# Expert-weighted token copies: the products split between VectorE and ScalarE, loads issued from within ScalarE's products, and half of the output stored in smaller pieces

## The chip, the cores and the metric

The kernel runs on one NeuronCore of a Trainium2 chip. The metric is the device time of one execution in microseconds (us). Thirteen runs of the kernel before gave a median of 240.83 us (240.25 to 242.64). The core has compute engines with their own instruction queues (the profile names them PE, DVE for VectorE, ACT for ScalarE, POOL, SP for SyncE) and 16 DMA engines that move data between HBM and the on-chip memory SBUF (128 partitions). A DMA is issued by an engine's queue; here SP and ScalarE issue all of them, and the profile shows their transfers as the DMA queues q1 (those issued by SP) and q10 (those issued by ScalarE).

## What is computed

Every token's hidden vector is copied k = 2 times, and each copy is multiplied by that slot's expert weight. The expert indices are not used.

```python
batch, seq, hidden, k = 16, 1024, 512, 2        # x, weights and output are float32
x_expanded = x[:, :, np.newaxis, :].repeat(k, axis=2)
weights = expert_weights[..., np.newaxis]
return (x_expanded * weights).astype(np.float32)
```

So 33.6 MB are read (x), 67.1 MB are written, and there is one multiplication per output element: 16,384 tokens by 2 slots by 512 elements.

## The kernel before, in words

The 16,384 tokens are taken in eight groups of 2,048. In a group, partition p holds 16 consecutive tokens (TX = 16), so that a load of a group is one DMA of 128 rows of 32 KB (4 MB in all, line 70), and one buffer of `x_tile` holds it. `x_pool` has two buffers. The weights of a group are a 128 x 32 block; all eight blocks are loaded ahead of everything else by eight small DMAs that SP issues (line 55; 16 KB each, in rows of 128 bytes), into one `w_tile`.

For each of the 16 tokens of a partition VectorE makes two products of shape 128 x 512 (line 83, a `tensor_scalar` multiplication whose scalar is a column of `w_tile`): one for slot 0, one for slot 1. They go into `o_tile`, which holds eight tokens (TO = 8) of 2 x 512 elements, 32 KB a partition. After eight tokens SP issues one store of that tile (line 91, 128 rows of 32 KB, 4 MB). `o_pool` has four buffers, so four stores can be outstanding. A whole run has 8 loads of x, 256 products and 16 stores.

The order is set by four things:

- VectorE works through the products in order. The first product of a group waits for that group's load; the first product of an output tile waits until the store that last used the buffer has landed.
- ScalarE's queue holds nothing but the eight loads (line 70). Load i+2 waits until VectorE has finished the products of group i, whose buffer it takes.
- SP's queue holds the eight weight loads and then the stores, in order. Each store waits for its tile's last product.
- The DMAs share eight completion semaphores, numbered 0 to 7 here, handed out in the order in which the scheduler places the DMAs. A DMA whose semaphore was used before waits until that earlier DMA has landed. So the eighth weight load waits for the first load of x, the second load of x waits for the first weight load, and the first stores wait for weight loads.

On each DMA engine a queue is worked through in its order, one row after another: a row of 32 KB is one packet in the trace. Where both queues have packets, the packets of the two alternate.

Of the kernel before, what the change touches and what calls it, by code (L numbers as in the profile page):

```python
# [1 line left out]

# [4 lines left out]


@with_exitstack
def kernel(  # L10
    ctx: ExitStack,
    tc: tile.TileContext,
    x: bass.AP,
    expert_indices: bass.AP,
    expert_weights: bass.AP,
    out: bass.AP,
):
    nc = tc.nc

    batch, seq, hidden = x.shape  # L20
    k = expert_weights.shape[-1]
    P = nc.NUM_PARTITIONS
    ntok = batch * seq
    assert ntok % P == 0
    A_TOTAL = ntok // P

    f32 = mybir.dt.float32
    row = k * hidden
    TX = 16
    TO = 8  # L30

    groups = [[[16]], [[16]], [[16]], [[16]], [[16]], [[16]], [[16]], [[16]]]
    assert sum(sum(sum(t) for t in g) for g in groups) == A_TOTAL

    xf = x.rearrange("b s h -> (b s) h")
    of = out.rearrange("b s k h -> (b s) (k h)")
    wf = expert_weights.rearrange("b s k -> (b s) k")

    w_pool = ctx.enter_context(tc.tile_pool(name="w_pool", bufs=1))
    x_pool = ctx.enter_context(tc.tile_pool(name="x_pool", bufs=2))
    o_pool = ctx.enter_context(tc.tile_pool(name="o_pool", bufs=4))

    w_tile = w_pool.tile([P, A_TOTAL * k], f32)

    def rows(of_all, done, T):
        return of_all[done * P : (done + T) * P, :].rearrange(
            "(p a) n -> p (a n)", a=T
        )  # L50

    done = 0
    for group in groups:
        T = sum(sum(t) for t in group)
        nc.sync.dma_start(
            out=w_tile[:, done * k : (done + T) * k], in_=rows(wf, done, T)
        )
        done += T

    done = 0  # L60
    for group in groups:
        T = sum(sum(t) for t in group)
        xr = rows(xf, done, T)
        outr = rows(of, done, T)
        a0 = 0
        for pieces in group:
            x_tile = x_pool.tile([P, TX * hidden], f32)
            at = 0
            for n in pieces:
                nc.scalar.dma_start(  # L70
                    out=x_tile[:, at * hidden : (at + n) * hidden],
                    in_=xr[:, (a0 + at) * hidden : (a0 + at + n) * hidden],
                )
                at += n
            ends = [sum(pieces[: i + 1]) for i in range(len(pieces))]
            first = 0
            for t in range(at):
                if t % TO == 0:
                    o_tile = o_pool.tile([P, TO * row], f32)
                for kk in range(k):  # L80
                    c = (done + a0 + t) * k + kk
                    o = t % TO * row + kk * hidden
                    nc.vector.tensor_scalar(  # L83
                        out=o_tile[:, o : o + hidden],
                        in0=x_tile[:, t * hidden : (t + 1) * hidden],
                        scalar1=w_tile[:, c : c + 1],
                        scalar2=None,
                        op0=mybir.AluOpType.mult,
                    )
                if t + 1 in ends or (t + 1) % TO == 0:  # L90
                    nc.sync.dma_start(
                        out=outr[:, (a0 + first) * row : (a0 + t + 1) * row],
                        in_=o_tile[:, first % TO * row : (t % TO + 1) * row],
                    )
                    first = t + 1
            a0 += at
        done += T


# [1 line left out]
_INS = ['x', 'expert_indices', 'expert_weights']  # L101
_OUTS = [((16, 1024, 2, 512), 'float32')]


# [23 lines left out]
```

## Time and profile before

| what | value |
|---|---|
| median of 13 runs | 240.83 us |
| time of the profiled execution | 240.83 us |
| its span, first to last instruction | 239.0 us |
| VectorE busy | 102.5 us, 43% of the span |
| one product, 128 x 512 | 481 ns; successive ones start 396 ns apart |
| bytes moved | 100.81 MB, mean 422 GB/s over the span |
| VectorE idle, waiting for stores to free a buffer | 74.9 us in 10 waits |
| VectorE idle, waiting for a load of x | 25.4 us in 2 waits |
| first product starts | 13.32 us |
| first store issued | 19.77 us |
| last store issued | 206.08 us |

How to read it: the span of one profiled execution lies 1.8 us below that execution's time, which is what lies around the first and last instruction. The time from an issue to the landing of a DMA holds its wait in the queue behind earlier DMAs as well as its own transfer: the median is 45.1 us for a store and 24.0 us for a load of x. The row of GB/s and the row of the DMA engines' busy share divide the span into 40 slices of 6 us.

### The profile page before, as it was taken

To read this page: it belongs to the slowest core of one execution; us is meant where nothing else is said; L and a number is where in the kernel's file an instruction comes from. 1 tells how busy PE (TensorE), PEld (TensorE's weight loads), DVE (VectorE), ACT (ScalarE), POOL (GpSimd) and SP (SyncE) were. 2 spreads that over 40 slices of the span, in tenths; PEclk is the share of its full clock that TensorE was granted. 3 is DMA by queue.
4 is the path that set the end of the run, shared out by engine and by line. 5 is a ranking of instruction groups with operands and counts; after the bars stand their busy time and mean duration, and the time that the engine had idled before them with its cause. 6 is when DMAs were issued, how large, how long until landed. Compare 5 with 4: busy or idle time off the path is not lost.

```text
span 239.0 us, 369 instructions
## 1 busy us (share of the span) xinstructions
DVE 102.5 (43%) x256; POOL 0.2 (0%) x4
## 2 busy tenths in 40 slices
DVE  0079994058700904672055910749008485400000
POOL 0000000000000000000000000000000000000000
DMA  7999999999999999999999999999999999999995
GB/s 266 440 440 400 417 429 389 433 439 439 433 422 433 422 439 439 439 428 433 428 439 433 439 428 439 439 435 422 433 422 428 439 433 428 439 433 439 433 439 225
DMA packets 4610, 100.81 MB, mean 422 GB/s; under 512 B 1536, under 2 KB 1536, under 8 KB 1536
## 3 DMA queue, kind: packets, MB, share of 16 engines
q1 hardware_dynamic: 3456, 67.24, 65.4%
q10 hardware_dynamic: 1152, 33.55, 33.2%
q14 instruction: 2, 0.02, 0.0%
HBM read 33.69 MB, written 67.11 MB: 422 GB/s over the span
## 4 chain that ended last, share of the span: by engine, by line
DMA 62%; DVE 18%; another core or an unknown queue 5%; issue 0%; DVEq 0%
DMA out_dram<-o_tile 56%; DVE o_tile L83 18%; DMA x_tile<-in_x_dram 5%; DVEq L123 0%; DVEq L83 0%
## 5 line engine op out<-in xcount | busy, mean ns | idle before, releaser
L83 DVE TENSOR_SCALAR o_tile<-x_tile,w_tile 128x512 f32<-128x512 f32 x256 | 102.5, 481 | 103.5 <-DMA out_dram<-o_tile 74.9
L112 POOL MEMSET const-bfloat16-1.0<- 128x1 bf16 x1 | 0.1, 101 | 0.0
L112 POOL MEMSET const-uint8-127<- 128x1 uint8 x1 | 0.1, 101 | 0.0
L112 POOL MEMSET const-float32-0.0<- 128x1 f32 x1 | 0.1, 98 | 0.2 <-issue 0.2
L112 POOL MEMSET const-float32-1.0<- 128x1 f32 x1 | 0.1, 98 | 0.0
## 6 DMA issues: line engine op xcount, KB each, us to landing
out_dram<-o_tile SPq DMA_DIRECT2D x16, 4096.0 KB, 45.1
x_tile<-in_x_dram ACTq DMA_DIRECT2D x8, 4096.0 KB, 24.0
w_tile<-in_expert_weights_dram SPq DMA_DIRECT2D x8, 16.0 KB, 20.7
```

The source lines that it names most:

```text
L83: nc.vector.tensor_scalar(out=o_tile[:, o : o + hidden], in0=x_tile[:, t * hidden : (t + 1) * hidden], scalar1=w_tile[:, c : c + 1], scala ...
L112: nc = _bacc.Bacc("TRN2", target_bir_lowering=False, num_devices=1)
```

## The change

Seven things are different in the new kernel:

- The product of slot 0 stays on VectorE (line 85), that of slot 1 is made by ScalarE (line 79, `nc.scalar.mul` with the same column of weights as its multiplier). Each has 128 products of 128 x 512. ScalarE also gets a load of its function table ahead of its first product.
- The 16 tokens of a group now go out in three stores in place of two: two of four tokens (128 rows of 16 KB, 2 MB each) and one of eight tokens (128 rows of 32 KB, 4 MB). There are 24 stores in place of 16.
- The pool of four 32 KB output buffers becomes a pool of four 16 KB buffers (`half_pool`) and a pool of two 32 KB ones (`o_pool`): the same bytes in all.
- The loads of x have the same size as before and are still issued by ScalarE, now with its products between them. The first two are issued at the start; load i+1 stands behind ScalarE's first product of group i.
- A load also waits for ScalarE's own products on the buffer it takes, and stores and buffers wait for both engines.
- With more DMAs, the eight completion semaphores fall to other DMAs. The first three stores now wait for the second, third and fifth weight load, and the next two for the sixth and eighth.
- The loops over lists of pieces are replaced by plain ones. The weight loads are as before.

```diff
     x_pool = ctx.enter_context(tc.tile_pool(name="x_pool", bufs=2))
-    o_pool = ctx.enter_context(tc.tile_pool(name="o_pool", bufs=4))
+    half_pool = ctx.enter_context(tc.tile_pool(name="half_pool", bufs=4))
+    o_pool = ctx.enter_context(tc.tile_pool(name="o_pool", bufs=2))
...
+    loaded = []
+    def load():
+        i = len(loaded)
+        if i < G:
+            loaded.append(x_pool.tile([P, TX * hidden], f32, name="x_tile"))
+            nc.scalar.dma_start(out=loaded[i], in_=rows(xf, i))
+    load()
+    load()
+    for i in range(G):
+        x_tile = loaded[i]
+        at = 0
+        for pool, m in ((half_pool, TO // 2), (half_pool, TO // 2), (o_pool, TO)):
+            o_tile = pool.tile([P, m * row], f32, name="o_tile")
+            for t in range(m):
                 for kk in range(k):
...
-                    nc.vector.tensor_scalar(
-                        out=o_tile[:, o : o + hidden],
-                        in0=x_tile[:, t * hidden : (t + 1) * hidden],
-                        scalar1=w_tile[:, c : c + 1],
-                        scalar2=None,
-                        op0=mybir.AluOpType.mult,
-                    )
-                if t + 1 in ends or (t + 1) % TO == 0:
-                    nc.sync.dma_start(
-                        out=outr[:, (a0 + first) * row : (a0 + t + 1) * row],
-                        in_=o_tile[:, first % TO * row : (t % TO + 1) * row],
-                    )
+                    if kk == 1:
+                        nc.scalar.mul(
+                            out=o_tile[:, o : o + hidden],
+                            in_=in_,
+                            mul=w_tile[:, c : c + 1],
+                        )
+                    else:
+                        nc.vector.tensor_scalar(
+                            out=o_tile[:, o : o + hidden],
+                            in0=in_,
+                            scalar1=w_tile[:, c : c + 1],
+                            scalar2=None,
+                            op0=mybir.AluOpType.mult,
+                        )
+                if i > 0 and at == 0 and t == 0:
+                    load()
+            nc.sync.dma_start(
+                out=rows(of, i)[:, at * row : (at + m) * row], in_=o_tile
+            )
+            at += m
```

More of the change, by code (lines that the diff above doesn't have):

```diff
@@ L30 @@
     TO = 8
-    groups = [[[16]], [[16]], [[16]], [[16]], [[16]], [[16]], [[16]], [[16]]]
-    assert sum(sum(sum(t) for t in g) for g in groups) == A_TOTAL
+    G = A_TOTAL // TX
+    assert A_TOTAL % TX == 0 and TX == 2 * TO
     xf = x.rearrange("b s h -> (b s) h")
@@ L42 @@
     x_pool = ctx.enter_context(tc.tile_pool(name="x_pool", bufs=2))
-    o_pool = ctx.enter_context(tc.tile_pool(name="o_pool", bufs=4))
-    w_tile = w_pool.tile([P, A_TOTAL * k], f32)
-    def rows(of_all, done, T):
-        return of_all[done * P : (done + T) * P, :].rearrange(
-            "(p a) n -> p (a n)", a=T
-        )
-    done = 0
-    for group in groups:
-        T = sum(sum(t) for t in group)
-        nc.sync.dma_start(
-            out=w_tile[:, done * k : (done + T) * k], in_=rows(wf, done, T)
-        )
-        done += T
@@ L60 @@
[L60 to L79, printed above, removed]
-                for kk in range(k):
-                    c = (done + a0 + t) * k + kk
-                    o = t % TO * row + kk * hidden
-                    nc.vector.tensor_scalar(
-                        out=o_tile[:, o : o + hidden],
-                        in0=x_tile[:, t * hidden : (t + 1) * hidden],
-                        scalar1=w_tile[:, c : c + 1],
-                        scalar2=None,
-                        op0=mybir.AluOpType.mult,
-                    )
-                if t + 1 in ends or (t + 1) % TO == 0:
-                    nc.sync.dma_start(
-                        out=outr[:, (a0 + first) * row : (a0 + t + 1) * row],
-                        in_=o_tile[:, first % TO * row : (t % TO + 1) * row],
[L94 to L97, printed above, removed]
@@ new lines, with rows @@
+    half_pool = ctx.enter_context(tc.tile_pool(name="half_pool", bufs=4))
+    o_pool = ctx.enter_context(tc.tile_pool(name="o_pool", bufs=2))
+    def rows(of_all, g):
+        return of_all[g * P * TX : (g + 1) * P * TX, :].rearrange(
+            "(p a) n -> p (a n)", a=TX
+        )
+    w_tile = w_pool.tile([P, A_TOTAL * k], f32)
+    for g in range(G):
+        nc.sync.dma_start(out=w_tile[:, g * TX * k : (g + 1) * TX * k], in_=rows(wf, g))
+    loaded = []
[4 more added lines that the diff above has]
+            nc.scalar.dma_start(out=loaded[i], in_=rows(xf, i))
@@ new lines @@
+    load()
[6 more added lines that the diff above has]
+            for t in range(m):
+                for kk in range(k):
+                    c = (i * TX + at + t) * k + kk
+                    o = t * row + kk * hidden
+                    in_ = x_tile[:, (at + t) * hidden : (at + t + 1) * hidden]
+                    if kk == 1:
[16 more added lines that the diff above has]
+                out=rows(of, i)[:, at * row : (at + m) * row], in_=o_tile
+            )
+            at += m
```

## The prediction

> **What bounds the kernel now.** I read the page's busy shares first, then the bandwidth by slices, then the waits, and last a table of stretches.
>
> ```profile
> span 239.0 us, 369 instructions
> DVE 102.5 (43%) x256; POOL 0.2 (0%) x4
> ...
> DMA  7999999999999999999999999999999999999995
> GB/s 266 440 440 400 417 429 389 433 439 439 433 422 433 422 439 439 439 428 433 428 439 433 439 428 439 439 435 422 433 422 428 439 433 428 439 433 439 433 439 225
> DMA packets 4610, 100.81 MB, mean 422 GB/s; under 512 B 1536, under 2 KB 1536, under 8 KB 1536
> q1 hardware_dynamic: 3456, 67.24, 65.4%
> q10 hardware_dynamic: 1152, 33.55, 33.2%
> DMA 62%; DVE 18%; another core or an unknown queue 5%; issue 0%; DVEq 0%
> ```
>
> The only computing engine is busy 43% of the time; the 16 DMA engines are busy in every slice but the first and last, and q1 and q10 together take 98.6% of them. The chain of waits puts 18% on VectorE, but only because it follows one thread back; while those products ran, the DMA engines were full with other stores. The waits agree: VectorE waits for DMAs.
>
> ```profile
> DVE o_tile L83 <- DMA out_dram<-o_tile: 74.9, 10, 12.9
> DVE o_tile L83 <- DMA x_tile<-in_x_dram: 25.4, 2, 13.3
> DVE o_tile L83 <- issue: 3.2, 1, 3.2
> ```
>
> The stretches (from:to, length, VectorE, POOL, clock, DMA share, GB/s) show where anything can be won:
>
> ```profile
> 0.00:4.00 4.00, 0.00 (x0) 0.20 (x4) 1.00 0.65 216
> 4.00:20.00 16.00, 6.68 (x17) 0.00 (x0) 1.00 1.02 436
> 20.00:25.00 5.00, 5.00 (x14) 0.00 (x0) 1.00 0.96 360
> 25.00:34.00 9.00, 9.00 (x24) 0.00 (x0) 1.00 1.03 445
> 34.00:39.00 5.00, 4.74 (x12) 0.00 (x0) 1.00 0.96 347
> 39.00:92.00 53.00, 19.27 (x48) 0.00 (x0) 1.00 1.00 433
> 102.00:180.00 78.00, 32.12 (x80) 0.00 (x0) 1.00 1.00 433
> 180.00:236.00 56.00, 19.27 (x48) 0.00 (x0) 1.00 1.00 432
> ```
>
> From 39 us to 236 us the rate is 432 to 433 GB/s, whether loads and stores are mixed (39 to 92) or stores run alone (180 to 236). That is the ceiling: 100.8 MB at 433 GB/s are 232.8 us, and the span is 239.0. The missing 6.2 us lie at the ends: about 2 us before full rate (0 to 4), 5 x (1 - 360/433) = 0.8 us in 20 to 25, 5 x (1 - 347/433) = 1.0 us in 34 to 39, 2.7 us after 236, less 0.4 us where the count of bytes by packets runs above the ceiling. The profiled execution's own time is 240.83 us, equal to the median of the 13 runs, so 1.83 us lie around the span and sums made on the span go over to the median unchanged.
>
> **The change, part by part.**
>
> *Slot 1 to ScalarE.* VectorE loses 128 of 256 products, 128 x 0.40 us (start to start) = 51 us of work. None was on the path: the DMA engines are full beside it. On ScalarE 128 products appear. The trace has no such row. A group's DMA work is 12.6 MB / 433 GB/s = 29.1 us and holds 16 of these products, so ScalarE becomes the bound only above 29.1/16 = 1.8 us each. From below, VectorE's 0.40 us for the same shape; from above, four times that, 1.6 us, a far end that I choose for want of a nearer row. I take the geometric mean, 0.8 us. Both ends are below 1.8, so the steady part costs 0. The table load stands behind the second load's issue (8.4 us) and ahead of the first product (13.3 us): it has 4.5 us of cover. The Trainium skill ("ScalarE: Activation LUTs", Rules for kernel authors) speaks against this part: multiplications belong on VectorE; by its figures, 280 ns plus 0.833 ns an element with one operand more read per partition, my estimate of a product is 0.71 us. By the skill a group takes 11.3 us on ScalarE and the sum would still be 0.
>
> *Loads behind products.* Before, load i+1 was issued when VectorE had finished group i-1 (38.77, 64.48, 99.60 us and so on). Now it stands behind ScalarE's first product of group i, which waits for load i and for the landing of the first half store of group i-2. At that moment the rest of group i-2 and all of group i-1 are still to be stored: 6.3 + 8.4 = 14.7 MB, 34 us of DMA time. A load that shares the engines takes the 24.0 us of its row, probably less, since its 32 KB packets now alternate with 16 KB ones in half of the stores. So the store queue never empties behind a late load: 0. Queued behind the waiting load's product on ScalarE are the other products of group i; they have the same 34 us of cover.
>
> *24 stores for 16.* SP's issues take 0.33 us each, 8 x 0.33 = 2.7 us more, on a queue that waits 177.8 us for VectorE: 0. What counts is the price on the DMA engines, which have no slack. The packet records of the trace give a median of 1213 ns for a 32,768-byte packet, 13 ns for a 128-byte one and 9 ns for a 4-byte semaphore write. A straight line through the first two gives 13 + 16,256 x 0.03676 = 611 ns for 16,384 bytes. Sixteen half stores have 128 such packets on each engine in place of 64 large ones: 128 x 611 - 64 x 1213 = 0.53 us, and eight more DMAs add eight semaphore writes: 0.07 us. Together +0.6 us. From below: exactly half a packet each, 0. From above: the weight loads that drain alone land 0.2 us apart with nine packets each (22.57, 22.77, 22.97, 23.19, 23.40 us for the first semaphore step of five of them), 22 ns a packet; 64 + 8 more packets at that price are 1.6 us. I take the line, because the large stream keeps its packets back to back and the small one did not. The Trainium skill ("DMA: Bandwidth & Descriptors", Anatomy of one DMA) speaks harder against it, with 2.0 us of fixed cost for every DMA: by that rule, laid end to end, eight more would cost 16 us. The trace contradicts it for queued DMAs: the last four 4 MB stores land 9.7 us apart (209.20, 218.87, 228.56, 238.23 us), and 4.19 MB at 433 GB/s are 9.69 us, which leaves no room for a fixed cost.
>
> *The head.* A half tile has its four products on ScalarE at about 13.3 + 4 x 0.8 = 16.5 us in place of 19.77. That brings nothing: in the trace of before no store packet moves until 22.53 us, though the first store was issued at 19.77, since the weight loads' small packets stand ahead of it on q1, alternating with 32 KB packets of x until those run out, from 22 us on. The first half store is then 8 x 0.61 = 4.9 us of DMA work on each engine, to 27.4 us at the earliest, where the 4 MB store before covered 9.7. The second half store has its products at 13.3 + 8 x 0.8 = 19.7 us but waits on the semaphore of the third weight load, which landed at 23.83 us: 3.6 us ahead of need. Then come the 4 MB store (fifth weight load, 24.18 us; products at 13.3 + 16 x 0.8 = 26.1 us) and the third load of x, behind ScalarE's first product of group 1 (about 26.9 us; before, 26.11). I cost the head at 0; its cover is this 3.6 us.
>
> *The tail.* The last store is again 4 MB and queued long before its turn. Ahead of it stand three stores of group 6 and two of group 7, 29 us of work, when its buffer comes free; its products need 8 x 0.8 = 6.4 us. 0.
>
> Sum: 240.83 + 0.6 = 241.4 us, +0.25%, with 0 to +1.6 from the packets.
>
> **Rivals.**
>
> *Dearer packets (slower).* The 16 KB packets cost the 22 ns overhead of the draining weight loads. For: that is the only row with many packets in a row. Against: they were tiny, and 32 KB packets at 433 GB/s leave no gap. 240.83 + 1.6 = 242.4 us. It decides from 10 ns a packet on, where the cost passes 0.3%.
>
> *The store queue runs dry in the head (slower).* A DMA that joins busy engines starts late: the third load was issued at 26.11 us and moved its first packet at 30.1. If the second half store needs the same 4.0 us, it starts at 27.8, 0.4 us after the first can end; if it starts only with the 4 MB store behind it (26.1 + 4.0 = 30.1), 2.7 us are lost. The middle, 1.6 us, gives with the packets 243.0. Against: on the same queue the next packets are fetched behind the running ones, and 19.77 to 22.53 was blocking, not latency.
>
> *ScalarE becomes the bound (slower).* Above 1.8 us a product; at 2.0 us each, 128 x 2.0 = 256 us plus a start of 13 and an end of 10: 279 us. Nothing in the trace speaks for it.
>
> *The head gets better (faster).* The dips of 20 to 25 and 34 to 39 us (0.8 + 1.0 us) are not explained by any wait: packets of x there took up to 2.3 us in place of 1.2. If they come from the pattern of 4 MB against 4 MB and vanish, 240.83 + 0.6 - 1.8 = 239.6 us. It decides once more than 1.3 us of the 1.8 are won. Against: similar slow packets come at the very start, where only loads run.
>
> **How the numbers follow.** My forecast has 0.56, dearer packets 0.19, a dry queue 0.09, ScalarE 0.03, the better head 0.13. A change under 0.3% (0.72 us) is about what a measurement of this kernel cannot tell from none. The forecast's own range is 240.8 to 242.0 (packets 0 to 1.2 us); of its 0.56 I put 0.13 above 241.55, where it counts as slower. So slower 0.13 + 0.19 + 0.09 + 0.03 = 0.44, same 0.43, faster 0.13. The range from 240.1 to 243.0 leaves out half of the better head, ScalarE, and some of the dry queue: under 2 in 10.
>
> **What will show it.** In the changed profile: 432 to 433 GB/s from 40 us to the last 3 us; 128 ScalarE products between 0.4 and 1.6 us; VectorE near 51 us of busy time start to start (61.6 at 481 ns each); the two large queue shares together still 98% or more; 16 KB packets at 611 ns. A slice below 8 tenths of DMA between 20 and 40 us would show the dry queue. I am wrong if the ceiling itself moves, for instance if 16 KB rows are written at another rate than 32 KB rows, since nothing in this trace wrote such rows.

## The result and the profile after

The changed kernel takes 244.89 us in the median (243.5 to 249.0) against 240.98 us (240.16 to 243.18) for the kernel before: a ratio of 1.0142, 95% interval 1.0115 to 1.0170. The ratio leaves out the run of 249.0 us, which is more than 1.5% above the fastest. The forecast was 241.4 us in a range of 240.1 to 243.0: the sign of the likeliest case was right, the size was not, and the median lies above the range. The profiled execution took 244.55 us with a span of 242.8; so 1.75 us lie around the span (1.83 before), and what is to be explained is 242.8 - 239.0 = 3.8 us of span.

The first lines of the changed kernel's page, its two computing engines, and its waits (engine, line, what was waited for: total us, times, longest):

```profile
span 242.8 us, 406 instructions
...
DVE 52.4 (22%) x128; ACT 81.8 (34%) x129; POOL 0.2 (0%) x4
...
DMA  7999999999999999999999999999999999999992
GB/s 267 428 434 351 443 440 413 443 432 418 400 470 431 439 432 397 440 405 437 410 424 440 421 427 397 429 448 432 437 410 432 454 413 429 454 413 429 454 432 108
...
q1 hardware_dynamic: 4608, 67.24, 65.1%
q10 hardware_dynamic: 1152, 33.55, 32.9%
...
L79 ACT ACT_TABLE_LOAD x1 | 1.3, 1283 | 8.7 <-DMA w_tile<-in_expert_weights_dram 8.7
```

```profile
L79 ACT ACTIVATE o_tile<-x_tile,w_tile 128x512 f32<-128x512 f32 x128 | 80.5, 709 | 117.7 <-DMA out_dram<-o_tile 113.5 <-DMA x_tile<-in_x_dram 4.0
```

```profile
DVE o_tile L85 <- DMA out_dram<-o_tile: 117.1, 12, 18.5
ACT o_tile L79 <- DMA out_dram<-o_tile: 113.5, 13, 17.6
```

Much of this is as foretold. The DMA engines are busy in every slice but the first and the last, the two large queues together take 98.0% of the 16 engines' span, and both computing engines wait for stores to free their buffers. A product takes 709 ns on ScalarE, and ScalarE is busy 34% of the time. No slice between 20 and 40 us falls below 9 tenths, so the store queue didn't run dry. Yet the same bytes need 3.8 us more.

Where they are lost is seen in the windows (from:to, length, VectorE, ScalarE where it computes, POOL, clock, DMA share, GB/s). Before:

```profile
0.00:25.00 25.00, 11.68 (x30) 0.20 (x4) 1.00 0.95 385
25.00:40.00 15.00, 13.74 (x35) 0.00 (x0) 1.00 1.01 411
40.00:180.00 140.00, 57.82 (x144) 0.00 (x0) 1.00 1.00 433
180.00:236.00 56.00, 19.27 (x48) 0.00 (x0) 1.00 1.00 432
236.00:239.00 3.00, 0.00 (x0) 0.00 (x0) 1.00 0.13 55
```

And after:

```profile
0.00:25.00 25.00, 7.52 (x19) 12.15 (x19) 0.20 (x4) 1.00 0.94 370
25.00:40.00 15.00, 5.33 (x14) 9.05 (x15) 0.00 (x0) 1.00 1.02 439
40.00:180.00 140.00, 29.68 (x72) 45.49 (x72) 0.00 (x0) 1.00 1.00 427
180.00:236.00 56.00, 9.86 (x24) 15.10 (x24) 0.00 (x0) 1.00 1.01 433
236.00:239.00 3.00, 0.00 (x0) 0.00 (x0) 0.00 (x0) 1.00 0.63 273
239.00:242.80 3.80, 0.00 (x0) 0.00 (x0) 0.00 (x0) 1.00 0.06 26
```

- *To 40 us nothing is lost.* Over the first 25 us the rates are 385 and 370 GB/s. With the 411 and 439 of the next 15 us that makes 9.63 + 6.17 = 15.8 MB before and 9.25 + 6.59 = 15.8 MB after.
- *From 40 to 180 us, while loads and stores share the engines, the rate falls from 433 to 427 GB/s* at a full DMA share: 140 x 6/433 = 1.9 us. The packets last longer; no engine is idle.
- *From 180 to 236 us, with stores alone, the ceiling is the old one,* 433 GB/s, although half of these bytes go out in 16 KB rows.
- *The end frays.* After 239.0 us, where the kernel before has finished, 3.8 us follow with 6% of the engines busy, on average one of 16. In the window before, 63% are busy.

So about half of the loss is lower throughput in the mixed stretch, and the other half is that the 16 engines do not finish together.

The trace also has a record of each packet. Summed up and divided by 16 they give microseconds of an average DMA engine. "Nominal" counts each long packet at its median (1213 ns for 32 KB, 611 ns for 16 KB). "Slow" is what packets took above that; where the text below adds up single slow packets, it counts those that took over 0.1 us too long. "Mean end" and "last end" are taken over the 16 completion writes of the last store, and their difference is "uneven".

| kernel | span | nominal | slow (stores, loads) | mean end | last end | uneven |
|---|---|---|---|---|---|---|
| before | 239.0 | 232.90 | 1.69 (0.09, 1.60) | 236.87 | 237.89 | 1.02 |
| after | 242.8 | 233.47 | 3.22 (1.06, 2.15) | 238.82 | 241.61 | 2.79 |

From before to after: packets +0.58 us, slow packets +1.53, uneven ends +1.77; what is left of the 3.7 us is -0.2. The first term is the 0.6 us of the prediction. The other two were not in it.

### The profile page after: what moved, and what is told of

Read it like the earlier page. It is cut to its first block, busy times and chain, and to the rows that moved or that the text cites. A ratio compares the mean times of both kernels' runs of the same rounds, so it can differ in the third digit from the quotient of the medians.

```text
span 242.8 us, 406 instructions
## 1 busy us (share of the span) xinstructions
DVE 52.4 (22%) x128; ACT 81.8 (34%) x129; POOL 0.2 (0%) x4
## 4 chain that ended last, share of the span: by engine, by line
DMA 47%; another core or an unknown queue 23%; ACT 15%; issue 1%; ACTq 1%
DMA out_dram<-o_tile 38%; ACT o_tile L79 15%; DMA x_tile<-in_x_dram 6%; DMA w_tile<-in_expert_weights_dram 3%; ACTq L60 0%; ACTq L122 0%
## 5 line engine op out<-in xcount | busy, mean ns | idle before, releaser
L79 ACT ACTIVATE o_tile<-x_tile,w_tile 128x512 f32<-128x512 f32 x128 | 80.5, 709 | 117.7 <-DMA out_dram<-o_tile 113.5
L85 DVE TENSOR_SCALAR o_tile<-x_tile,w_tile 128x512 f32<-128x512 f32 x128 | 52.4, 481 | 154.1 <-DMA out_dram<-o_tile 117.1
L79 ACT ACT_TABLE_LOAD x1 | 1.3, 1283 | 8.7 <-DMA w_tile<-in_expert_weights_dram 8.7
```

The costliest lines, as they stand in the source:

```text
L79: nc.scalar.mul(out=o_tile[:, o : o + hidden], in_=in_, mul=w_tile[:, c : c + 1],)
L85: nc.vector.tensor_scalar(out=o_tile[:, o : o + hidden], in0=in_, scalar1=w_tile[:, c : c + 1], scalar2=None, op0=mybir.AluOpType.mult,)
```

## The experiments

The change has two parts that can be made one by one: the two short stores a group ("pieces"), and ScalarE's work with the loads issued behind its products ("split" and "gate"). All the kernels below compute the whole output. Ratios are to the kernel before on the same chip, with 95% intervals.

### The parts one at a time

**pieces_only**: the changed stores, all products on VectorE, and each load issued without a product of ScalarE ahead of it.

```diff
-                    if kk == 1:
+                    if False:
...
-                if i > 0 and at == 0 and t == 0:
-                    load()
...
             at += m
+        load()
```

> Only the 16 KB pieces are kept: three stores a group from the new pools, all 256 products on VectorE, loads issued by a ScalarE queue that holds nothing else. In the changed kernel's trace the 16 KB packets took 611 ns, as the line said, so 0.6 us of its 3.7 us of longer span are explained; the rest are packets that ran slower than their kind (3.2 us a DMA engine in place of 1.7) and DMA engines that ended up to 2.8 us behind the mean of the sixteen in place of 1.0. Theory 'pieces' (the half-size packets bring the slow packets and the uneven ends): ratio 1.012 to 1.017 to the kernel before, about 244.5 us. Theory 'gate' (loads held back behind a product that waits for a store's buffer, so that they enter at other moments): 1.000 to 1.004, about 241.6 us. Theory 'ScalarE' (128 products on a second engine disturb the transfers): the same, about 241.6 us.

Measured: 243.71 us, 1.0088 [1.0055, 1.0122]. The pieces alone, with no work on ScalarE, make the kernel slower by 0.88%, of which the packets' own 0.58 us are 0.24%. That lies between the two forecasts: too much for 'gate' and 'ScalarE' (up to 1.004), and only the upper end of the interval reaches that of 'pieces' (from 1.012).

**gate_only**: 32 KB stores; ScalarE makes only the first product of each group, and the load stands behind that (`issue_after` orders it behind the instruction named).

```diff
-                    if kk == 1:
-                        nc.scalar.mul(
+                    if kk == 1 and at + t == 0:
+                        gate = nc.scalar.mul(
...
-        for pool, m in ((half_pool, TO // 2), (half_pool, TO // 2), (o_pool, TO)):
+        for pool, m in ((o_pool, TO), (o_pool, TO)):
...
-                    load()
+                    with tc.issue_after(gate):
+                        load()
```

> 32 KB stores as before, two a group; ScalarE makes one product a group (the first token's slot 1) and issues the next load behind it; the other 248 products are on VectorE. Theory 'pieces': 1.000, about 240.9 us. Theory 'gate': 1.010 to 1.016, about 244 us. Theory 'ScalarE': 1.000, since eight products are nothing beside 128.

Measured: 247.05 us, 1.0248 [1.0208, 1.0288]. This run doesn't test the gate. The first store was issued only at 25.90 us, after 31 products of VectorE, where the kernel before issued it at 19.77. In the trace the first store on SP's queue waits for VectorE alone, so it is that of the second tile; the first tile's, which also waits for ScalarE, stands behind it (26.34 us). The page's DMA row, and the windows around it (columns as above):

```profile
DMA  7996799999999999999999999999999999999991
```

```profile
20.00:22.00 2.00, 2.00 (x6) 0.00 (x0) 0.00 (x0) 1.00 0.81 346
22.00:27.00 5.00, 5.00 (x14) 0.72 (x1) 0.00 (x0) 1.00 0.53 123
27.00:29.00 2.00, 2.00 (x7) 0.00 (x0) 0.00 (x0) 1.00 0.65 262
```

The engines miss 2 x 0.19 + 5 x 0.47 + 2 x 0.35 = 3.4 us here. It is the "store queue runs dry" rival made real by accident, and it shows what that rival looks like: a 6 in the DMA row. The changed kernel has none. One engine of this run also ended 3.5 us after the mean; whether the gap in the head is the reason was not tested.

**split_and_gate**: everything of the change but the pieces.

```diff
-    half_pool = ctx.enter_context(tc.tile_pool(name="half_pool", bufs=4))
-    o_pool = ctx.enter_context(tc.tile_pool(name="o_pool", bufs=2))
+    o_pool = ctx.enter_context(tc.tile_pool(name="o_pool", bufs=4))
...
-        for pool, m in ((half_pool, TO // 2), (half_pool, TO // 2), (o_pool, TO)):
+        for pool, m in ((o_pool, TO), (o_pool, TO)):
```

> The changed kernel with 32 KB stores (two a group, four buffers): all slot-1 products on ScalarE and the loads behind its first product of a group. Theory 'pieces': 1.000, about 240.9 us. Theory 'gate': 1.010 to 1.016. Theory 'ScalarE': 1.010 to 1.016; gate_only tells the last two apart.

Measured: 240.21 us, 0.9967 [0.9945, 0.9989]. ScalarE's 128 products, its table load and the gated loads cost nothing; with 32 KB stores they leave the kernel slightly faster than before. The forecasts of 'gate' and 'ScalarE' (1.010 to 1.016) fell. The engines end more evenly (0.53 us between mean and last, 1.02 before).

**pieces_and_gate**: the changed kernel with only the first product of each group on ScalarE.

```diff
-                    if kk == 1:
+                    if kk == 1 and at + t == 0:
...
-                    load()
+                    with tc.issue_after(gate):
+                        load()
```

> The changed kernel with only the first slot-1 product of each group left on ScalarE, the rest on VectorE: pieces and gate without the bulk of ScalarE's work. Theory 'pieces': 1.012 to 1.017. Theory 'gate': 1.010 to 1.016. Theory 'ScalarE': 1.003, about 241.6 us.

Measured: 244.51 us, 1.0158 [1.0086, 1.0231], like the whole change. The other 120 products on ScalarE are not needed for the loss, and pieces with gated loads are enough. Whether the gate adds to what the pieces do alone is not settled by this, since the interval (1.0086 to 1.0231) overlaps that of pieces_only (1.0055 to 1.0122). SP's order differs here too: the 32 KB store of the first group (25.7 us) stands ahead of one of its 16 KB stores (26.1 us).

### Short rows as such, or two lengths side by side?

The next four kernels share one edit, which brings the weights in two DMAs in place of eight. uniform_32k is split_and_gate with this edit alone and is the one the others are to be compared with.

```diff
-    for g in range(G):
-        nc.sync.dma_start(out=w_tile[:, g * TX * k : (g + 1) * TX * k], in_=rows(wf, g))
+    nc.sync.dma_start(out=w_tile[:, : TX * k], in_=rows(wf, 0))
+    nc.sync.dma_start(
+        out=w_tile[:, TX * k :].rearrange("p (g n) -> p g n", g=G - 1),
+        in_=wf[P * TX :, :].rearrange("(g p a) k -> p g (a k)", p=P, a=TX),
+    )
```

> split_and_gate (32 KB stores, 32 KB loads, slot 1 on ScalarE) with the weights in two DMAs in place of eight: group 0, then the other seven groups together. It is the base of the three other runs of this set. Two theories of what the pieces do. 'Mixing': as long as all long packets have one length, the 16 DMA engines keep their phases to each other and no packet is slow; with two lengths the phases shift and packets collide. 'Small stores': 16 KB store packets are slow by themselves. Both expect here what split_and_gate gave or a little less, ratio 0.990 to 0.998: no packets slower than 1213 ns after 40 us, engine ends within 1.2 us of their mean.

Measured: 241.70 us, 1.0013 [0.9984, 1.0042], above the 0.990 to 0.998 expected. Its ends are as even as expected (1.1 us between mean and last), but its loads lose 12.0 us in slow packets after 40 us (summed over the engines), where those of the kernel before lose 0.8 and those of split_and_gate 0.4. Why was not examined.

**stores_16k**: all stores in 16 KB rows, loads in 32 KB rows.

```diff
-    o_pool = ctx.enter_context(tc.tile_pool(name="o_pool", bufs=4))
+    half_pool = ctx.enter_context(tc.tile_pool(name="half_pool", bufs=8))
...
-        for pool, m in ((o_pool, TO), (o_pool, TO)):
+        for pool, m in ((half_pool, TO // 2),) * 4:
```

> As uniform_32k, but every store is a 16 KB piece (32 stores, eight 16 KB buffers), loads in 32 KB rows. Packets alone: 64 x 1.213 + 256 x 0.611 = 234.1 us an engine, 1.1 more than with 32 KB only. Both theories: slower than that, since lengths are mixed wherever a load runs beside stores; 'mixing' 1.005 to 1.015 with the disturbance confined to the stretches with a load in them, 'small stores' 1.015 to 1.03 and slow store packets also where stores run alone.

**all_16k**: the same, and each load in two halves of 16 KB rows. **loads_16k**: 32 KB stores and only the loads in halves.

```diff
-            nc.scalar.dma_start(out=loaded[i], in_=rows(xf, i))
+            for h in range(2):
+                n = TX // 2 * hidden
+                nc.scalar.dma_start(
+                    out=loaded[i][:, h * n : (h + 1) * n],
+                    in_=rows(xf, i)[:, h * n : (h + 1) * n],
+                )
```

> As uniform_32k, but every long packet is 16 KB: stores in 16 KB pieces and each load as two DMAs of 16 KB rows. Packets alone: 384 x 0.611 = 234.6 us an engine, 1.7 more than with 32 KB only. Theory 'mixing': only these 1.7 us, ratio 1.000 to 1.006, hardly a slow packet after 40 us, engine ends within 1.2 us of their mean. Theory 'small stores': as stores_16k or worse, 1.015 to 1.03.

> As uniform_32k, but each load is two DMAs of 16 KB rows; stores keep 32 KB. Packets alone: 128 x 1.213 + 128 x 0.611 = 233.5 us, 0.6 more, the same mix of bytes in long and short packets as in the changed kernel. Theory 'mixing': slow packets while a load runs and uneven ends, ratio 1.003 to 1.013. Theory 'small stores': 0.993 to 1.001, no more slow packets than uniform_32k.

Measured: stores_16k 245.65 us, 1.0182 [1.0118, 1.0247]; all_16k 244.45 us, 1.0141 [1.0084, 1.0198]; loads_16k 243.13 us, 1.0062 [1.0024, 1.0100]. Twice as many short stores do not double the loss of the change. The idea that it comes only from two lengths beside each other fell: all_16k, with one length throughout, is 1.3% above uniform_32k. Of this the packets' own price (1.7 us) is 0.7%, and the intervals alone would not exclude that nothing is left; but its stores lose 11.4 us in slow packets after 40 us and its ends lie 2.6 us apart from their mean, where 'mixing' foretold hardly a slow packet and 1.2 us. Nor can 16 KB stores be slow wherever they run, since with stores alone the windows show 431 to 433 GB/s (180 to 236 us) in stores_16k, all_16k and the changed kernel. The first two:

```profile
40.00:180.00 140.00, 30.05 (x72) 46.07 (x72) 0.00 (x0) 1.00 1.00 424
180.00:236.00 56.00, 10.05 (x24) 15.36 (x24) 0.00 (x0) 1.00 1.01 431
```

```profile
40.00:180.00 140.00, 30.19 (x73) 48.33 (x75) 0.00 (x0) 1.00 1.01 429
180.00:236.00 56.00, 8.37 (x20) 12.79 (x20) 0.00 (x0) 1.00 1.01 431
```

loads_16k went the way of 'mixing' (1.003 to 1.013) and against 'small stores' (0.993 to 1.001). Its 32 KB stores lose 6.2 us in slow packets after 40 us, none of them over 0.45 us too long and almost none near a load's first packet, and its ends lie 2.3 us apart from their mean. So neither theory covers all three runs, and uneven ends also come with whole stores beside short load rows.

### Two queues or one

**one_queue_32k** issues the loads from SP as well, behind the stores of a group, so that loads and stores never alternate. **one_queue_16k** is the same with the pieces of the change. Both bring the weights in two DMAs, that of group 0 ahead of the first load and the other between the first two loads.

```diff
-            nc.scalar.dma_start(out=loaded[i], in_=rows(xf, i))
+            nc.sync.dma_start(out=loaded[i], in_=rows(xf, i))
...
-                if i > 0 and at == 0 and t == 0:
-                    load()
...
             at += m
+        load()
```

> The same single queue with two 32 KB stores a group. Both theories: no slow packets after 40 us; ratio 0.993 to 1.000, and 0.6 us below one_queue_16k by 'entry', 2.5 to 4 us below it by 'short rows'. If the two queues were what keeps the DMA engines full, it would be above 1.01 instead.

> The changed kernel with every DMA on SP's queue, in the order weights of group 0, first load, other weights, second load, then three stores and a load by turns, so that no load ever enters beside running stores. In the runs so far, slow store packets after 40 us add up to 9 to 16 us (summed over the 16 DMA engines) with 16 KB stores and to 0.4 to 1.0 us with 32 KB stores, and nearly all of them lie within 2.5 us of a load's first packet. Theory 'entry' (a load that enters beside 16 KB stores slows single store packets on some engines to half speed, and these engines end late): no such packets here, engine ends within 1.3 us of their mean, ratio 0.996 to 1.004, the 0.6 us of longer packets included. Rival 'short rows' (16 KB stores drift apart by themselves): still 1.010 to 1.018 and ends 2.3 us or more apart from the mean.

Measured: 243.13 us, 1.0068 [1.0039, 1.0098] with 32 KB rows, and 243.05 us, 1.0070 [1.0037, 1.0103] with the pieces. Both lie above what was expected (0.993 to 1.000 and 0.996 to 1.004). Their difference is what counts here: on one queue the pieces cost nothing that can be measured (1.0002, with both intervals combined 0.996 to 1.005; in packets alone they would be 0.24%), and the 16 KB packets lose only 0.7 us after 40 us (the 32 KB packets, loads and stores together, 13.5 us, against 17.3 with 32 KB rows alone). So eight more DMAs and 1,024 more packets are not what makes the change slow: it takes loads on the other queue, which run beside the short stores. (One queue costs 0.7% against the kernel before; the records show packets slowed by up to 0.3 us an engine at a switch between loading and storing, but that these make it up was not tested.)

**halves_by_partition** is uniform_32k with more DMAs and no shorter rows: the first store of each group as two DMAs of 64 partitions.

```diff
+            cuts = (0, P // 2, P) if at == 0 else (0, P)
+            for p0, p1 in zip(cuts, cuts[1:]):
-            nc.sync.dma_start(
-                out=rows(of, i)[:, at * row : (at + m) * row], in_=o_tile
-            )
+                nc.sync.dma_start(
+                    out=rows(of, i)[p0:p1, at * row : (at + m) * row],
+                    in_=o_tile[p0:p1, :],
+                )
```

> As uniform_32k, but the first store of each group is two DMAs of 64 partitions: 24 stores as in the changed kernel, every long packet 32 KB. Theories 'entry' and 'short rows': as uniform_32k, 0.995 to 1.004. Rival 'more DMAs' (24 stores with their semaphores are what costs): 1.010 to 1.018.

Measured: 327.04 us (318.4 to 332.1) against 241.03. It brought another effect, far larger than the one in question. Its page:

```profile
span 322.8 us, 387 instructions
...
DMA  8999999999999999999999999999999999754210
GB/s 327 432 361 284 390 382 443 333 382 382 426 416 382 240 272 374 374 313 276 353 296 370 398 337 284 325 414 410 313 317 292 317 300 288 227 187 118 73 53 32
```

The engines are full, yet the rate drops below 300 GB/s in several slices of the first 190 us; single store packets took up to 8.8 us, and the 16 engines ended between 290 and 321 us. Eight more DMAs with whole rows are thus untested by it; one_queue_16k answers for their count, on one queue.

### The moment at which a load enters

What is left is the meeting of a load with short stores. After 40 us the stores of the changed kernel lose 15.7 us in slow packets (summed over the 16 engines), 15.2 of them within 2.5 us of a load's first packet; with 32 KB stores they lose 0.4 (before) and 0.5 (split_and_gate). The figure varies from run to run: the same kernel traced once more (changed_again, below) loses 6.3. The worst entry of the first trace, as the packet records have it, an extract (start us, queue, bytes, duration ns; q1 stores, q10 loads):

```
101.11 q1  16384   611
101.21 q1  16384   755
101.28 q1  16384   753
101.34 q1  16384   776
101.72 q10 32768  1213
101.73 q1  16384  1024
101.99 q1  32768  2382
102.00 q1  32768  2320
102.14 q1  32768  2296
```

The load enters just where the stores pass from 16 KB to 32 KB rows. In the 1.5 us ahead of the load's first packet 29 short and 8 long store packets start: the engines are on different rows. About 16 long packets are in flight at a time, one on each engine; some of them take almost twice their time and others do not.

**later_entry** leaves all instructions as they are and issues each load four tokens later, behind ScalarE's first product of the second half store.

```diff
-                        nc.scalar.mul(
+                        product = nc.scalar.mul(
...
-                        )
+                        ).ins
...
-                if i > 0 and at == 0 and t == 0:
-                    load()
+                if i > 0 and at == TO // 2 and t == 0:
+                    with tc.issue_after(product):
+                        load()
```

It ran on one chip together with **split_and_gate_again** and **changed_again**, which are the kernels split_and_gate and the changed one once more.

> The changed kernel with each load moved from behind ScalarE's first product of a group to behind its first product of the second half tile. It then waits for the landing of the second half store of two groups before, so that its first packets run beside the 32 KB store that follows and not at the seam of 16 and 32 KB packets. Packets, pieces and products are the same. Theory 'entry': the slow store packets after 40 us fall from 15.7 us (summed over 16 DMA engines) to under 5, engine ends within 1.5 us of their mean, ratio 1.000 to 1.007. Rival 'pieces wherever two queues alternate' (the entry is only where the slow packets happen to show): still 1.010 to 1.018. A load that comes too late would show as empty slices and a ratio above 1.02.

> split_and_gate once more, the same kernel, beside the changed kernel on the same chip: 0.994 to 0.999 if its gain of 0.3% is real; 0.999 to 1.002 if it was the draw of the runs.

> The changed kernel once more, on the same chip as split_and_gate_again, which differs from it in the pieces alone: 1.012 to 1.017. The quotient of the two is the price of the pieces on two queues: 1.0142 / 0.9967 = 1.0176 from the separate runs, and 1.015 to 1.020 is expected here.

Measured: later_entry 241.86 us, 1.0025 [0.9999, 1.0052]; split_and_gate_again 240.08 us, 0.9960 [0.9939, 0.9981]; changed_again 244.07 us, 1.0116 [1.0079, 1.0153]. The first two lie in the ranges of 'entry' and of a real gain, the third just under the 1.012 to 1.017 expected. From 40 us on, the windows of later_entry:

```profile
40.00:180.00 140.00, 32.75 (x80) 48.68 (x78) 0.00 (x0) 1.00 1.00 429
180.00:236.00 56.00, 6.80 (x17) 11.96 (x20) 0.00 (x0) 1.00 1.01 433
236.00:239.00 3.00, 0.00 (x0) 0.00 (x0) 0.00 (x0) 1.00 0.48 208
239.00:242.80 3.80, 0.00 (x0) 0.00 (x0) 0.00 (x0) 1.00 0.00 0
```

And of split_and_gate_again:

```profile
40.00:180.00 140.00, 32.59 (x80) 49.47 (x79) 0.00 (x0) 1.00 1.01 434
180.00:236.00 56.00, 6.52 (x16) 10.74 (x18) 0.00 (x0) 1.00 1.00 432
236.00:239.00 3.00, 0.00 (x0) 0.00 (x0) 0.00 (x0) 1.00 0.00 0
```

The frayed end, the last 3.8 us at 6% (2% in changed_again), is gone with later entries; the mixed stretch has recovered only from 427 to 429 GB/s. The records, in the columns of the first table:

| kernel | span | nominal | slow (stores, loads) | mean end | last end | uneven |
|---|---|---|---|---|---|---|
| changed_again | 241.6 | 233.47 | 2.94 (0.53, 2.41) | 238.47 | 240.47 | 1.99 |
| later_entry | 240.0 | 233.47 | 2.39 (0.30, 2.09) | 238.15 | 238.81 | 0.66 |
| split_and_gate_again | 238.2 | 232.90 | 1.30 (0.07, 1.23) | 236.57 | 237.10 | 0.53 |
| pieces_and_gate | 243.1 | 233.47 | 2.52 (0.67, 1.84) | 237.98 | 241.94 | 3.96 |
| stores_16k | 244.9 | 234.05 | 3.80 (0.92, 2.87) | 239.96 | 243.66 | 3.71 |

On this chip the price of the pieces in the changed kernel is 1.0116/0.9960 = 1.0157, with both intervals combined about 1.011 to 1.020, or 3.8 us. It splits so: 244.07 - 241.86 = 2.2 us go when the loads enter later; the packets' own price is 0.58 us; some 1.0 us is left, and later_entry's slow packets exceed split_and_gate_again's by 1.1 us, most of it in loads. Against changed_again what fell with the later entry is above all the uneven end (1.99 to 0.66 us); slow packets fell by 0.55 us, and the stores' part of them after 40 us, summed over the engines, from 6.3 to 4.1 us. So on this chip the slow store packets are the smaller part of what later entries win back.

split_and_gate beats both kernels, by 0.33% and 0.40% against the one before, both intervals below 1. Why it beats it is not settled; the profiles show ends closer together (0.53 us for 1.02) and fewer slow packets. Most of the latter are load packets of the first 40 us, which lose 1.54 us an engine before, 1.39 in split_and_gate and 1.21 in split_and_gate_again.

What stays open is why a packet takes up to twice its time when a load enters, and on which engines. That the entry falls on a change of row length is not the whole answer. In later_entry all five entries after 40 us fall among 32 KB packets alone and cost the stores 0 to 3.2 us of slow time (summed over the engines); but in pieces_only an entry at 103.3 us among 32 KB packets alone costs 4.9, and in the changed kernel one at 72.5 us, among 33 short and 8 long ones, costs nothing. Loads lose as well: after 40 us their slow packets sum to 11.5 us in the changed kernel, 16.2 in changed_again and 13.4 in later_entry, but also to 12.0 in uniform_32k, where all long rows are 32 KB.

## Why the prediction was wrong, step by step

- *What bounds the kernel: right.* The DMA engines are full before and after.
- *Slot 1 to ScalarE, 0: right.* A product takes 709 ns, inside the bounds of 400 to 1600 and far below the 1.8 us at which ScalarE would decide. split_and_gate, with all 128 products there, is no slower than before. The table load took 1283 ns, inside its cover of 4.5 us. The estimate from the Trainium skill ("ScalarE: Activation LUTs", What ACT_TABLE_LOAD costs, where its figures per instruction and element stand), 0.71 us, is what the trace shows (709 ns).
- *24 stores for 16, +0.6 us: the failed step.* Its packets were right: a 16 KB packet has a median of 611 ns, the number taken from the straight line, and the sum of packets rose by 0.58 us (128 x 611 - 64 x 1213 is 0.58 us, not the 0.53 of the prediction). But the term took the packets' own time for the whole price of the short stores, and left out what they meet on the other queue. On one chip, with ScalarE's products and the gate in both kernels, the pieces cost 3.8 us (changed_again against split_and_gate_again); without the gate they cost 0.88%, 2.1 us (pieces_only); with the loads on the same queue, nothing measurable (one_queue_16k). The 2.0 us a DMA of the Trainium skill ("DMA: Bandwidth & Descriptors", Anatomy of one DMA), by the prediction's estimate 16 us in all, were nowhere: one_queue_16k, with its eight more stores, is at the time of one_queue_32k. That section gives the figure for DMAs issued by GpSimd; here SP issued the stores.
- *The head, 0: right.* By 40 us both kernels have moved 15.8 MB, and there is no gap.
- *Loads behind products, 0: right beside whole stores, not beside short ones.* With 32 KB stores the gated loads cost nothing (split_and_gate, 0.9967); beside the pieces, moving only the loads by four tokens takes back 2.2 us of the 3.8. The step asked only whether a late load would starve the stores, and none did. It took for granted that a packet keeps its duration whatever it meets and that 433 GB/s hold in the mixed stretch. Beside the short stores they do not: 427 GB/s between 40 and 180 us, +1.5 us of slow packets. The prediction said it would be wrong "if the ceiling itself moves" and named 16 KB rows as such a case; the ceiling did move, but not because of the rows alone (433 GB/s in the same rows without loads, 180 to 236 us). It gave that case no chance and no price. Why packets slow down there stays open.
- *The tail, 0: another half of the same loss.* The last store was queued in time (208.21 us), as argued. But the sum treated the 16 engines as one. The time is that of the last of them, 241.6 us where the mean is 238.8. The ends come apart by 1.8 us more than before. That slow packets on some of the engines cause it is argued, not shown. In one trace each, both shrink when the loads enter later (uneven 1.99 to 0.66 us, store time in slow packets 0.53 to 0.30); but loads_16k ends unevenly (2.3 us) with no store packet over 0.45 us too long.
- *Rivals.* Dearer packets (22 ns each) fell: 611 ns. A dry queue fell: no slice in the head below 9 tenths, and gate_only shows what one looks like. ScalarE as the bound fell. The better head fell for the changed kernel with the equal 15.8 MB. With whole stores a little of it is seen: of split_and_gate_again's 0.8 us of shorter span, about 0.3 are fewer slow load packets before 40 us.

The range failed since its upper end was made from two prices, dear packets and a dry head. A lower rate in the mixed stretch and uneven ends, each worth some 1.8 us, stood nowhere in it, though the trace of before had both in small: 1.7 us of slow packets and 1.0 us between the mean and the last engine's end.

## What to carry to other kernels

In a kernel whose DMA engines are full throughout, a change in the size of rows or in the moment of a transfer is not free when it is hidden: price the packets, then ask what each new transfer meets on the other queue, and give the case that packets slow down there a chance and a price (here 1.5 us of 240). Read the end of the trace by engine and not as a mean: here half of the loss was that some of the 16 engines finished late. Before splitting a store to start it earlier, look whether the DMA engines have a gap that the earlier start would fill; here they had none, and the same change with whole stores was the fastest version of all (0.9960).

## What the runs showed of the hardware that was not expected

- When a load enters on the other queue beside 16 KB stores, in the changed kernel's first trace single store packets took 1024 ns for 611 and 2382 ns for 1213, while others at the same moment kept their time. Before and in split_and_gate such slow store packets sum to 0.4 and 0.5 us over all 16 engines after 40 us, in the changed kernel to 15.7 in one trace and 6.3 in another.
- Two stores of 64 partitions each in place of one of 128, once a group, raised the time from 241 to 327 us, with packets of up to 8.8 us.
- Loads and stores on one queue, never alternating, took 0.7% longer than the kernel before (1.0068), where one might expect one direction at a time to run best; uniform_32k, with the same products and rows on two queues, is at 1.0013.
